# A hybrid decoder layer: its first piece projected by kinds of parts, with keys taken out whole by ScalarE and x in another bank

## Chip, cores and metric

One core of one Trainium2 chip runs the kernel. The metric is the device time of one launch in microseconds: the median of several runs. Profiles are of one execution each, whose time is longer than an unprofiled run's.

## What is computed

One decoder layer over 1024 positions plus 16 meta tokens in front (1040 rows), width 1024, all in float32:

```python
h = concatenate([meta, x])                       # 1040 x 1024
u = rmsnorm(h, g_pre_mix)
q, k, v, xr, yr = split(u @ w_in)                # 512, 128, 128, 512, 512 columns
attn = sliding_window_attention_with_sinks(q, k, v)   # 8 heads, 2 key heads, window 128
hr = rg_lru(causal_depthwise_conv(xr))           # gates, then a scan over time
mix = concatenate([attn, gelu(yr) * hr]) @ w_out
h = h + rmsnorm(mix, g_post_mix)
u = rmsnorm(h, g_pre_ffn)
f = square(relu(u @ w_ff1)) @ w_ff2
out = (h + rmsnorm(f, g_post_ffn))[16:]
```

## The kernel before

**Products in parts.** TensorE multiplies a rounded float32 type. Each operand is therefore kept as two tiles: a high part, which is the value rounded (ScalarE, L95 for weights, L116 for u), and a low part, which is what the rounding left off (VectorE, L98 and L117). A product is three matmuls into the same bank (`mm3`, L123 to L125): high by high, high weight by low u, low weight by high u. The next operation on a bank is its take-out ("sink"): keys, values, queries and x each have one.

**The start.** The rows of h come in as nine tiles: 16 meta rows, then x by 128. `norm_rows` squares a tile on ScalarE with a running sum (L200), GpSimd makes the reciprocal root (L158, L164), VectorE scales the tile (L202). `transposed(b, ...)` turns two such tiles (and meta) into eight blocks of u: TensorE transposes (L242) into a bank of one of the pools pt, o and s in turn, and `split_scaled` writes high and low part (L116, L117). There are four pieces b of 272, 256, 256 and 256 positions. For each piece `project` multiplies with the weights of keys, values, the first query pair and the first x chunk, eight blocks of width times three matmuls each, in a bank of the pool acc:

```python
for b in range(4):
    if b:
        transposed(b, normed(b))
    piece = [ALL[b]]
    project(wk, piece, sink_k)
    project(wv, piece, sink_v)
    project(wq, piece if b else [(16, 256)], sink_q0)
    project(wx, piece, sink_x0)
```

Each pool (acc, s, pt, o) holds two banks. A third use waits until the first is taken out. The keys' take-out (`put_k`, L303 to L305) does, for each of two heads, a copy on ScalarE and a copy and a difference on VectorE; in the first piece it is done once for the 16 meta positions (tile km) and once for the rest.

**After the start.** Attention runs head pair by head pair: scores (reduction on VectorE L467, exponential on ScalarE L82), reciprocals and scalings (L478, L480), transposes of the probabilities (L495) and their high and low parts (L95, L98), products with the values (L506) and their sums (L520, L521). Between them stand "fills": the projections of the other query pairs and of x chunks 1 to 3, which ScalarE copies out by pieces (L339). A chunk's causal convolution is four operations on VectorE (L530, three times L535). Tiles live in slots by tag; the x chunks and their convolutions share the four slots of tag d, so a new chunk's first copy waits for the release of its slot. The gates' weights are loaded into a tile that GpSimd clears first (L604) and four DMAs then fill (L608). Then follow gates, recurrence, output projection and the feed-forward part.

**What sets the order.** The program is written in the order of the source, but the framework's scheduler (`schedule_with_timeline_sim=True`) places the instructions on each engine by priority and its own estimate of times. `behind(name, ins)` adds an order without a semaphore between two instructions of an engine. SP issues the loads in the order that the source has them: meta, two x tiles, gains, weights of keys, values, queries, two x tiles, weights of x, the other x tiles, then small parameters and the next weights.

## Time and profile before

| | |
|---|---|
| median of 3 runs | 974.11 us (974.01 to 975.25) |
| profiled execution | 979.5 us |
| its span, first to last instruction | 977.7 us |
| mean granted TensorE clock | 0.994 |
| TensorE, VectorE, ScalarE, GpSimd busy | 98%, 70%, 51%, 7% of the span |

A row of the timeline is start and duration in us, engine, line, operation, what it writes and reads (buffer numbers left out), its shape and how often it stands there; in brackets the idle time ahead of it and what ended that. PE is TensorE's matmuls, PEld its weight loads, DVE is VectorE, ACT ScalarE, POOL GpSimd, SP the queue that issues most DMAs. Instructions of an engine overlap a little, so the distance of two starts is the price of one in a row, and the duration the time until its result.

### The profile page before, as it was taken

The numbers are of one execution on the slowest core, as the hardware profiler recorded it, in microseconds if no ns is written. First come the engines' busy times: TensorE is split into PE (matmuls) and PEld (weight loads), VectorE is DVE, ScalarE is ACT, GpSimd is POOL, SyncE is SP. The second block draws the span as 40 slices with busy tenths as digits, with TensorE's granted clock in tenths as the row PEclk, the third lists the DMA queues.
The fourth block names the chain that finished last, engine by engine and source line by source line (L and its number), as shares of the span: only waits on it lengthen the run. The fifth ranks groups of instructions, "written<-read, shape, count | busy, mean of one in ns | idle before, by whom it ended". The sixth has DMA issues, their size and how long they took to land.

```text
span 977.7 us, 12515 instructions
## 1 busy us (share of the span) xinstructions
PE 953.8 (98%) x4782; PEld 802.8 (82%) x4782; DVE 680.3 (70%) x1002; ACT 502.4 (51%) x809; POOL 70.4 (7%) x108
## 2 busy tenths in 40 slices
PE   6999999999999999999999999999999999999985
PEld 5999999888878877888888888888888888888874
DVE  6679997765976696675654465476668677779686
ACT  7557673558844664443555565663433444344331
POOL 4100000000011100000000000000111000002012
PEclk9999999999999999999999999999999999999998
DMA  8102101112134457586523364324777766657762
GB/s 275 42 2 65 23 22 44 37 43 73 65 130 155 160 181 236 173 264 191 170 93 103 107 194 129 108 86 129 169 167 182 213 211 200 192 151 197 213 173 86
DMA packets 89371, 133.28 MB, mean 136 GB/s; under 512 B 13752, under 2 KB 52680, under 8 KB 89312
## 3 DMA queue, kind: packets, MB, share of 16 engines
q1 hardware_dynamic: 81488, 112.04, 36.0%
q0 software_dynamic: 6960, 18.35, 8.9%
q10 hardware_dynamic: 864, 2.10, 0.6%
q8 instruction: 37, 0.61, 0.3%
q14 instruction: 22, 0.18, 0.1%
HBM read 113.60 MB, written 18.87 MB: 135 GB/s over the span
## 4 chain that ended last, share of the span: by engine, by line
PE 88%; DVE 5%; DMA 4%; ACT 1%; issue 1%; SPq 0%; POOLq 0%; DVEq 0%; POOL 0%; ACTq 0%
PE ps_acc L124 11%; PE ps_acc L125 11%; PE ps_acc L123 11%; PE ps_s L123 6%; PE ps_s L125 6%; PE ps_s L124 6%; PE ps_pt L123 6%; PE ps_pt L125 6%; PE ps_pt L124 6%; PE ps_o L123 5%; PE ps_o L124 5%; PE ps_o L125 5%; DMA raw<-in_w_ff_dram 3%; PE ps_o L506 2%; PE ps_pt L495 1%; DVE c L650 1%
## 5 line engine op out<-in xcount | busy, mean ns | idle before, releaser
L95 ACT CAST ws<-raw 128x1024 fp32r<-128x1024 f32 (+1 forms) x70 | 71.7, 1024 | 131.2 <-PE ps_o L124 39.8
L98 DVE TENSOR_TENSOR ws<-raw,ws 128x1024 fp32r<-128x1024 f32 (+1 forms) x71 | 84.7, 1194 | 52.7 <-ACT ws L95 52.6
L123 PE MATMUL ps_acc<-a,ws 128*128 128x256 f32 (+2 forms) x272 | 90.5, 333 | 0.6 <-DVE b L305 0.6
L124 PE MATMUL ps_acc<-a,ws 128*128 128x256 f32 (+2 forms) x272 | 89.7, 330 | 0.0
L125 PE MATMUL ps_acc<-a,ws 128*128 128x256 f32 (+2 forms) x272 | 89.4, 329 | 0.0
L95 ACT CAST ws<-e 128x1024 fp32r<-128x1024 f32 x44 | 46.0, 1047 | 61.0 <-PE ps_o L124 28.2
L98 DVE TENSOR_TENSOR b<-b,b 128x1024 fp32r<-128x1024 f32 (+2 forms) x48 | 57.6, 1201 | 25.0 <-PE ps_o L124 17.5
L98 DVE TENSOR_TENSOR ws<-e,ws 128x1024 fp32r<-128x1024 f32 x44 | 53.8, 1223 | 20.3 <-ACT ws L95 20.3
L95 ACT CAST b<-b 128x1024 fp32r<-128x1024 f32 (+2 forms) x48 | 49.4, 1030 | 35.7 <-DVE b L789 33.7
L123 PEld LDWEIGHTS ps_acc<-a,ws 128*128 128x128 f32 x272 | 51.2, 188 | 4.9 <-DVE b L305 0.8
L125 PEld LDWEIGHTS ps_acc<-a,ws 128*128 128x128 f32 x272 | 51.2, 188 | 4.6
L124 PEld LDWEIGHTS ps_acc<-a,ws 128*128 128x128 f32 x272 | 51.2, 188 | 3.9
L123 PE MATMUL ps_acc<-ws,b 128*128 128x512 f32 (+1 forms) x120 | 46.6, 388 | 2.1 <-ACT ws L95 2.1
L124 PE MATMUL ps_acc<-ws,b 128*128 128x512 f32 (+1 forms) x120 | 46.8, 390 | 0.8 <-DVE ws L98 0.8
L125 PE MATMUL ps_acc<-ws,b 128*128 128x512 f32 (+1 forms) x120 | 46.6, 388 | 0.0
L164 POOL TENSOR_TENSOR rs<-ms,half_pow 128x1 f32<-128x1 f32 (+1 forms) x31 | 20.9, 677 | 348.6 <-DVE ms L160 347.2
L123 PE MATMUL ps_pt<-ws,b 128*128 128x512 f32 x112 | 44.1, 394 | 0.0
L124 PE MATMUL ps_pt<-ws,b 128*128 128x512 f32 x112 | 44.1, 394 | 0.0
L125 PE MATMUL ps_pt<-ws,b 128*128 128x512 f32 x112 | 44.0, 393 | 0.0
L123 PE MATMUL ps_s<-ws,b 128*128 128x512 f32 x110 | 43.7, 397 | 0.0
L124 PE MATMUL ps_s<-ws,b 128*128 128x512 f32 x110 | 43.4, 395 | 0.0
L125 PE MATMUL ps_s<-ws,b 128*128 128x512 f32 x110 | 43.3, 393 | 0.0
(375 smaller groups left out, 2676.3 us busy)
## 6 DMA issues: line engine op xcount, KB each, us to landing
raw<-in_w_ff_dram SPq DMA_DIRECT2D x66, 512.0 KB, 3.8
e<-in_w_ff_dram SPq DMA_DIRECT2D x47, 512.0 KB, 3.8
d<-in_w_ff_dram SPq DMA_DIRECT2D x12, 512.0 KB, 4.0
s_dram<-d POOLq DMA_DIRECT2D x12, 512.0 KB, 3.9
raw<-in_w_in_dram SPq DMA_DIRECT2D x9, 512.0 KB, 3.8
raw<-in_w_ff_dram POOLq DMA_DIRECT2D x9, 512.0 KB, 8.0
c<-in_x_dram SPq DMA_DIRECT2D x8, 512.0 KB, 8.6
d<-in_x_dram SPq DMA_DIRECT2D x8, 512.0 KB, 4.5
```

The source lines that it names most:

```text
L95: nc.scalar.copy(hi, src)
L98: low = nc.vector.tensor_tensor(lo, src, f32(hi), op=ALU.subtract).ins
L123: nc.tensor.matmul(dst, lh, rh, start=start, stop=False, skip_group_check=True)
L124: nc.tensor.matmul(dst, lh, rl, start=False, stop=False, skip_group_check=True)
L125: nc.tensor.matmul(dst, ll, rh, start=False, stop=stop, skip_group_check=True)
L164: nc.gpsimd.tensor_tensor(rs[:n], ms[:n], half_pow[:n], op=ALU.pow)
L495: nc.tensor.transpose(pt[:, o : o + P], sn[h][:, 2 * bp + i, s * P : (s + 1) * P], ident,)
L506: nc.tensor.matmul(po[:, oc : oc + n], v, p_[:, pc : pc + n], start=first and k == 0, stop=last and k == 1, skip_group_check=True,)
L650: nc.vector.tensor_tensor_scan(r, av[c], gi, 0.0, op0=ALU.mult, op1=ALU.add)
```

## The change

- The first piece's keys and values are projected by kinds: the keys' eight blocks of high weight by high u, then their eight of high weight by low u, the same two kinds for the values, and only then low weight by high u for both (new function `part`). Queries and x of the first piece follow in the same three kinds, each on its own. The other pieces keep `project`.
- The x projection of the first piece uses a bank of pool s instead of acc. The transposes use the pools as before.
- ScalarE and VectorE each get a fixed order for the first piece (`chained`). ScalarE: high part of the key weights, the eight high parts of u, high part of the value weights, the squares of the next two x tiles, of the query weights; then the keys' take-out, the values', the x weights. VectorE: the eight low parts of u, low parts of key and value weights, the two scalings, low part of the query weights, the keys' take-out, low part of the x weights.
- `put_k` has both ScalarE copies first, then VectorE's four operations; the queries' take-out likewise.
- The tiles khh and kl are made, and kl's halves cleared by GpSimd, ahead of the start's loop.
- The transposes of the later pieces get an order behind the last matmul of an earlier piece through `after`: `done` begins with two empty entries, so piece 1 has none, piece 2 comes behind the first piece's last matmul and piece 3 behind the second's.
- The clearing of the gates' tile comes behind GpSimd's last reciprocal root of the start.

The instructions themselves are the same ones: 4782 matmuls, as many operations on the other engines.

```diff
--- before.py
+++ after.py
@@ -113,16 +113,21 @@
             )
 
     def split_scaled(hi, lo, src, scale):
-        nc.scalar.activation(hi, src, AF.Copy, scale=scale)
-        nc.vector.scalar_tensor_tensor(
+        high = nc.scalar.activation(hi, src, AF.Copy, scale=scale).ins
+        low = nc.vector.scalar_tensor_tensor(
             lo, src, scale, f32(hi), op0=ALU.mult, op1=ALU.subtract
-        )
+        ).ins
+        return high, low
 
     def mm3(dst, lhs, rhs, start, stop):
         (lh, ll), (rh, rl) = lhs, rhs
         nc.tensor.matmul(dst, lh, rh, start=start, stop=False, skip_group_check=True)
         nc.tensor.matmul(dst, lh, rl, start=False, stop=False, skip_group_check=True)
-        nc.tensor.matmul(dst, ll, rh, start=False, stop=stop, skip_group_check=True)
+        last_mm[0] = nc.tensor.matmul(
+            dst, ll, rh, start=False, stop=stop, skip_group_check=True
+        ).ins.name
+
+    last_mm = [None]
 
 
     ident = const.tile([P, P], F32, name="ident")
@@ -161,8 +166,12 @@
                 ms[:n], ssq_parts[0], EPS, ssq_parts[1], op0=ALU.add, op1=ALU.add
             )
         rs = small.tile([P, 1], F32, name="rs", tag="rs")
-        nc.gpsimd.tensor_tensor(rs[:n], ms[:n], half_pow[:n], op=ALU.pow)
+        last_pow[0] = nc.gpsimd.tensor_tensor(
+            rs[:n], ms[:n], half_pow[:n], op=ALU.pow
+        ).ins.name
         return rs[:n]
+
+    last_pow = [None]
 
 
     def load_cols(cols, tag="ws"):
@@ -194,12 +203,18 @@
     u = [pair("a", [P, TT]) for _ in range(KC)]
     RMS_SC = 1.0 / math.sqrt(D)
 
-    def norm_rows(src, n):
+    def norm_rows(src, n, link=False):
         xn = slot("d", [P, D])
         ssq = small.tile([P, 1], F32, name="ssq", tag="ssq")
-        nc.scalar.activation(xn[:n], src, AF.Square, scale=RMS_SC, accum_out=ssq[:n])
+        ins = nc.scalar.activation(
+            xn[:n], src, AF.Square, scale=RMS_SC, accum_out=ssq[:n]
+        ).ins
+        if link:
+            chained(0, ins)
         rs = rstd_of([ssq[:n]], n)
-        nc.vector.tensor_scalar(xn[:n], src, rs, None, op0=ALU.mult)
+        ins = nc.vector.tensor_scalar(xn[:n], src, rs, None, op0=ALU.mult).ins
+        if link:
+            chained(1, ins)
         return xn
 
     def project(w, pieces, sink):
@@ -215,8 +230,26 @@
                 )
             sink(acc[:, :n], t0, n)
 
+
+    def part(acc, w, piece, k, last=2):
+        t0, n = piece
+        for kc in range(KC):
+            last_mm[0] = nc.tensor.matmul(
+                acc[:, :n], w[k // 2][:, kc, :], u[kc][k % 2][:, t0 : t0 + n],
+                start=k == 0 and kc == 0, stop=k == last and kc == KC - 1,
+                skip_group_check=True,
+            ).ins.name
+
     ALL = [(0, 272), (272, 256), (528, 256), (784, 256)]
     REAL2 = [(16, 512), (528, 512)]
+
+
+
+    khh = [slot("b", [P, T], F32R) for _ in range(2)]
+    kl = [slot("b", [P, T], F32R) for _ in range(2)]
+    HALF = (slice(0, HD), slice(HD, P))
+    for h in range(2):
+        nc.gpsimd.memset(f32(kl[h][HALF[1 - h]]), 0.0)
 
     zero = slot("ws", [P, 512])
     nc.vector.memset(zero, 0.0)
@@ -232,22 +265,43 @@
         rows += [(xt[2 * b], P), (xt[2 * b + 1], P)]
         return [(norm_rows(s[:m], m), m) for s, m in rows]
 
-    def transposed(b, xn):
+
+    last = [None, None]
+
+    def chained(e, ins):
+        if last[e] is not None:
+            behind(last[e], ins)
+        last[e] = ins.name
+
+    def high_w(raw, tag="ws"):
+        hi, lo = pair(tag, [P, KC, P])
+        chained(0, nc.scalar.copy(hi, raw).ins)
+        return hi, lo
+
+    def low_w(w, raw):
+        chained(1, nc.vector.tensor_tensor(w[1], raw, f32(w[0]), op=ALU.subtract).ins)
+
+    def transposed(b, xn, after=None):
         t0, n = ALL[b]
         for kc in range(KC):
             flip[0] += 1
             pt = bank(("pt", "o", "s")[flip[0] % 3])
             o = 0
             for s, m in xn:
-                nc.tensor.transpose(
+                ins = nc.tensor.transpose(
                     pt[:, o : o + m], s[:m, kc * P : (kc + 1) * P], ident[:m, :m]
                 )
+                if after:
+                    behind(after, ins.ins)
                 o += m
             uh, ul = u[kc]
-            split_scaled(
+            high = split_scaled(
                 uh[:, t0 : t0 + n], ul[:, t0 : t0 + n], pt[:, :n],
                 g_mix_col[:, kc : kc + 1],
             )
+            if b == 0:
+                chained(0, high[0])
+                chained(1, high[1])
 
     def fetch(cols, tag="raw"):
         raw = slot(tag, [P, KC, P])
@@ -274,11 +328,14 @@
     rx = fetch([(X_COL, P)], "e")
     for i in range(4, 8):
         load_x(i)
-    wk = split_w(rk, "b")
-    wv = split_w(rv, "b")
+    wk = high_w(rk, "b")
     transposed(0, xn)
-    wq = split_w(rq)
-    wx = split_w(rx)
+    low_w(wk, rk)
+    wv = high_w(rv, "b")
+    low_w(wv, rv)
+    xn = [(norm_rows(xt[i], P, True), P) for i in (2, 3)]
+    wq = high_w(rq)
+    low_w(wq, rq)
     nsink = const.tile([P, 8], F32, name="nsink")
     nc.sync.dma_start(nsink, attn_sinks[0].partition_broadcast(P))
     prm_r = slot("d", [8, 512])
@@ -287,38 +344,45 @@
         nc.sync.dma_start(prm_r[4 + i : 5 + i, :], src)
 
 
-
-    khh = [slot("b", [P, T], F32R) for _ in range(2)]
-    kl = [slot("b", [P, T], F32R) for _ in range(2)]
-
     vk = [slot("b", [P, 8, P], F32R) for _ in range(2)]
-    HALF = (slice(0, HD), slice(HD, P))
     vt = slot("c", [P, TT])
-    for h in range(2):
-        nc.gpsimd.memset(f32(kl[h][HALF[1 - h]]), 0.0)
-
-    def put_k(hh, lo, src):
+
+    def put_k(hh, lo, src, link=False):
+        ops = [[], []]
+        for h in range(2):
+            r = HALF[h]
+            ops[0].append(nc.scalar.copy(hh[h][r], src[r]).ins)
         for h in range(2):
             r, o = HALF[h], HALF[1 - h]
-            nc.scalar.copy(hh[h][r], src[r])
-            nc.vector.tensor_copy(hh[h][o], src[r])
-            nc.vector.tensor_tensor(lo[h][r], src[r], f32(hh[h][r]), op=ALU.subtract)
+            ops[1].append(nc.vector.tensor_copy(hh[h][o], src[r]).ins)
+            ops[1].append(
+                nc.vector.tensor_tensor(
+                    lo[h][r], src[r], f32(hh[h][r]), op=ALU.subtract
+                ).ins
+            )
+        if link:
+            for e in range(2):
+                for ins in ops[e]:
+                    chained(e, ins)
 
     def sink_k(acc, t0, n):
         o = 0
         if t0 == 0:
             m = slice(0, NMETA)
             put_k(
-                [km[:, 0, m], km[:, 1, m]], [km[:, 2, m], km[:, 3, m]], acc[:, m]
+                [km[:, 0, m], km[:, 1, m]], [km[:, 2, m], km[:, 3, m]], acc[:, m], True
             )
             o = NMETA
         c = slice(t0 + o - NMETA, t0 - NMETA + n)
         put_k(
-            [khh[0][:, c], khh[1][:, c]], [kl[0][:, c], kl[1][:, c]], acc[:, o:]
+            [khh[0][:, c], khh[1][:, c]], [kl[0][:, c], kl[1][:, c]], acc[:, o:],
+            t0 == 0,
         )
 
     def sink_v(acc, t0, n):
-        nc.scalar.copy(vt[:, t0 : t0 + n], acc)
+        ins = nc.scalar.copy(vt[:, t0 : t0 + n], acc).ins
+        if t0 == 0:
+            chained(0, ins)
 
     def new_q():
 
@@ -327,8 +391,14 @@
         def sink_q(acc, t0, n):
             c = slice(t0 - NMETA, t0 - NMETA + n)
             for h in range(2):
+                r = HALF[h]
+                nc.scalar.activation(q[h][r, c], acc[r], AF.Copy, scale=HD ** -0.5)
+            for h in range(2):
                 r, o = HALF[h], HALF[1 - h]
-                split_scaled(q[h][r, c], q[h][o, c], acc[r], HD ** -0.5)
+                nc.vector.scalar_tensor_tensor(
+                    q[h][o, c], acc[r], HD ** -0.5, f32(q[h][r, c]),
+                    op0=ALU.mult, op1=ALU.subtract,
+                )
 
         return q, sink_q
 
@@ -340,16 +410,39 @@
 
         return xr, sink_x
 
+
+    done = [None, None]
     q0, sink_q0 = new_q()
     xr0, sink_x0 = new_x("c")
     for b in range(4):
         if b:
-            transposed(b, normed(b))
-        piece = [ALL[b]]
-        project(wk, piece, sink_k)
-        project(wv, piece, sink_v)
-        project(wq, piece if b else [(16, 256)], sink_q0)
-        project(wx, piece, sink_x0)
+            transposed(b, xn if b == 1 else normed(b), done[b])
+        piece = ALL[b]
+        if b == 0:
+
+            acc = [bank("acc"), bank("acc")]
+            for a, w in zip(acc, (wk, wv)):
+                part(a, w, piece, 0)
+                part(a, w, piece, 1)
+            for a, w, sink in zip(acc, (wk, wv), (sink_k, sink_v)):
+                part(a, w, piece, 2)
+                sink(a[:, : piece[1]], *piece)
+            wx = high_w(rx)
+            low_w(wx, rx)
+            for w, (t0, n), sink, tag in (
+                (wq, (16, 256), sink_q0, "acc"), (wx, piece, sink_x0, "s")
+            ):
+                acc = bank(tag)
+                for k in range(3):
+                    part(acc, w, (t0, n), k)
+                sink(acc[:, :n], t0, n)
+            done.append(last_mm[0])
+            continue
+        project(wk, [piece], sink_k)
+        project(wv, [piece], sink_v)
+        project(wq, [piece], sink_q0)
+        project(wx, [piece], sink_x0)
+        done.append(last_mm[0])
 
 
     prm = const.tile([P, NLRU, 8], F32, name="prm")
@@ -601,7 +694,7 @@
 
 
     graw = slot("e", [P, 2, NLRU, P])
-    nc.gpsimd.memset(graw, 0.0)
+    behind(last_pow[0], nc.gpsimd.memset(graw, 0.0).ins)
     for i, w in enumerate((w_a, w_x)):
         for s in range(2):
             r = slice(HD * s, HD * s + HD)
```

## The prediction

> **What bounds the kernel now.** I read the busy table first, then TensorE's waits over the whole span, then busy time by stretches, then the timelines of the two places that the change moves. In the waits the columns are the total in us, the number of times and the longest; in the stretches each engine's busy us and instruction count stand in the order PE, PEld, DVE, ACT, POOL, then clock, DMA share and GB/s.
>
> ```profile
> PE 953.8 (98%) x4782; PEld 802.8 (82%) x4782; DVE 680.3 (70%) x1002; ACT 502.4 (51%) x809; POOL 70.4 (7%) x108
> ```
> ```profile
> PE ps_s L242 <- DVE d L202: 5.7, 1, 5.7
> ...
> PE ps_acc L123 <- DVE b L305: 0.6, 1, 0.6
> ```
> ```profile
> 82.00:147.25 65.25, 65.25 (x497) 62.33 (x497) 60.54 (x172) 45.20 (x117) 0.00 (x0) 1.00 0.10 25
> 147.25:156.21 8.96, 8.96 (x79) 8.91 (x78) 8.07 (x9) 2.95 (x8) 0.00 (x0) 1.00 0.21 60
> 156.21:250.00 93.79, 93.79 (x513) 81.92 (x512) 62.07 (x112) 59.13 (x106) 0.00 (x0) 1.00 0.16 46
> ```
>
> TensorE is the bound: 98% busy, and from 82 to 250 us it is never idle, though VectorE is nearly as full between 82 and 156 (60.54 of 65.25 us). So a microsecond of TensorE idle time removed anywhere shortens the span by about as much, and one added lengthens it. What can be gained lies in the start. The change cannot make TensorE's work smaller: the same 4782 matmuls remain.
>
> A second fact decides more than the edits themselves. The kernel's order on each engine is made by a scheduler from priorities. In the changed program TensorE's order differs from the old one up to about matmul 1350 of 4782 (some 200 us) and is the same from there on. So I cost two places: the start, where the edits are, and the rest of those 200 us, where only the order moves.
>
> **The start, part by part.** Rows of the timeline (start, duration, engine, line), the first x rows and key weights, then the second piece:
>
> ```profile
> 7.60 0.75 DVE L202 TENSOR_SCALAR d<-c,rs 128x1024 f32<-128x1024 f32 x1
> 9.06 1.05 ACT L95 CAST b<-raw 128x1024 fp32r<-128x1024 f32 x1 [1.20 <-DMA raw<-in_w_in_dram]
> 9.12 1.52 DVE L202 TENSOR_SCALAR d<-c,rs 128x1024 f32<-128x1024 f32 x1 [0.77 <-POOL rs L164]
> 9.14 2.38 POOL L298 MEMSET b<- 64x1024 f32 x2
> 10.56 2.34 DVE L98 TENSOR_TENSOR b<-raw,b 128x1024 fp32r<-128x1024 f32 x2
> 11.49 0.48 ACT L116 ACTIVATE a<-ps_o,gcol 128x272 fp32r<-128x272 f32 x1
> 11.88 0.48 ACT L116 ACTIVATE a<-ps_s,gcol 128x272 fp32r<-128x272 f32 x1
> 13.24 0.49 DVE L117 SCALAR_TENSOR_TENSOR a<-ps_s,gcol,a 128x272 fp32r<-128x272 f32 x1
> 13.64 0.49 DVE L117 SCALAR_TENSOR_TENSOR a<-ps_pt,gcol,a 128x272 fp32r<-128x272 f32 x1
> 14.53 0.43 PE L123 MATMUL ps_acc<-a,b 128*128 128x272 f32 x1
> 14.75 0.43 PE L124 MATMUL ps_acc<-a,b 128*128 128x272 f32 x1
> 15.88 1.06 ACT L200 ACTIVATE d<-c 128x1024 f32<-128x1024 f32 x1 [0.70 <-PE ps_s L242]
> 18.03 0.75 DVE L202 TENSOR_SCALAR d<-c,rs 128x1024 f32<-128x1024 f32 x1
> 18.37 0.29 PE L124 MATMUL ps_acc<-a,b 128*128 128x272 f32 x1
> 18.49 0.30 PE L125 MATMUL ps_acc<-a,b 128*128 128x272 f32 x1
> ```
> ```profile
> 19.29 1.07 ACT L200 ACTIVATE d<-c 128x1024 f32<-128x1024 f32 x1
> 21.45 0.17 DVE L304 CAST km<-ps_acc 64x16 fp32r<-64x16 f32 x1
> 22.20 0.75 DVE L202 TENSOR_SCALAR d<-c,rs 128x1024 f32<-128x1024 f32 x1 [0.41 <-POOL rs L164]
> 27.23 0.43 DVE L305 TENSOR_TENSOR b<-ps_acc,b 64x256 fp32r<-64x256 f32 x1
> 21.38 0.29 PE L125 MATMUL ps_acc<-a,b 128*128 128x272 f32 x1
> 21.51 0.27 PE L242 MATMUL ps_pt<-ident,d 128*128 128x128 f32 x1
> 21.62 0.27 PE L242 MATMUL ps_o<-ident,d 128*128 128x128 f32 x1
> 22.74 0.36 PE L123 MATMUL ps_acc<-a,ws 128*128 128x256 f32 x1
> 25.53 0.28 PE L125 MATMUL ps_acc<-a,ws 128*128 128x256 f32 x1
> 27.72 0.39 PE L123 MATMUL ps_acc<-a,ws 128*128 128x272 f32 x1 [0.57 <-DVE b L305]
> ```
>
> *Memsets of the key tiles go to the very start of GpSimd's queue.* Today they lie beside the second x row's normalisation, which takes 1.52 us where the first took 0.75. Alone it ends at 9.87 instead of 10.64: 0.77 us earlier. In their new place they stand ahead of the identity and of meta's rstd, which VectorE must have behind it only by 7.60; 2.38 us more on a queue that started at the span's begin leave cover for that, and if it were gone, each microsecond would move the whole start by one. The gates' memset goes behind the eighth rstd; the gate weights' four small DMAs wait for it on SP, and behind them later weight loads. I cost that at nothing: all x rows and the first piece's weights are issued before them, and the attention's projections stand between them and the gates.
>
> *Work by kinds.* ScalarE now does the key weights, then eight high parts of u in a row, and only then the value weights. First high part at about 10.4 instead of 11.49; at a pitch of 0.39 the eight end near 13.6. VectorE does its eight low parts (pitch 0.40) near 10.9 to 14.3 and only then the two weights' low parts (2.34 in all), to 16.6. The value weights' high part is there at 13.6 + 1.05 = 14.6. TensorE takes all 32 products with high weights first (the keys' 16 to about 15.7 at the slow pace of 0.22, 14.53 to 14.75; the values' 16 to about 18.2 while the pace rises to 0.12, 18.37 to 18.49), then the 16 with low weights, 2.0, to 20.2. The old kernel starts its last one at 21.38. Here 1.2 us are won.
>
> *Then it meets a new wait.* The x projection takes its bank from the pool of transposes, and the order that results sends TensorE from eight transposes of the second piece (four banks, near 21.0) straight to one that reuses the first of those banks. That bank is free when VectorE has taken u's low part from it. Ahead of that on VectorE's queue stand: the third and fourth x rows' normalisation, the queries' low weights, four small key copies and the fifth row's normalisation. The third row's square starts at 15.88 in the trace (ScalarE is free from 14.6, but no view shows its data landed sooner), its normalisation 2.15 later (15.88 to 18.03); the fourth's 1.07 behind, 19.1 to 19.9; low weights 1.17, to 21.1; four copies at 0.17, to 21.8; the fifth's normalisation (its square starts at 19.29 and VectorE at 22.20 today; I take 22.0) to 22.7; low part 0.49, to 23.2. TensorE waits some 2 us, then 0.4 more for the next bank, and starts the queries near 23.8, against 22.74 today: +1.1. Both kernels have twelve transposes done there. Behind TensorE's wait stand the queries and all that follows. On ScalarE the fifth square stands ahead of the keys' copies and the second piece's high parts; it lets them go at 20.4, while their transposes are being made.
>
> *The old pause goes.* Today TensorE's last query matmul starts at 25.53 and x starts at 27.72, 2.19 later; 0.12 of that is a matmul and eight transposes at 0.11 (21.51 to 21.62) are work, so 1.19 is idle time, ended by the keys' take-out (L305). With its bank elsewhere x follows at once: -1.2. VectorE's key take-out, four steps of 0.43 to about 26, is then covered by the query and x products (48 at 0.12 = 5.8 us); without this cover it would cost its own 1.7. ScalarE's two copies ahead of VectorE's four change only the order.
>
> Sum of the start: +1.1 - 1.2 = -0.1. Bounds: -1.2 if the new wait is fully absent, +1.3 if the pause is merely moved.
>
> **The rest of the 200 us.** One place shows a price. x chunk 3 is written into the slot that x chunk 2 occupies until its convolution (L530, three times L535) is done. ScalarE's first copy of chunk 3 (L339) waits for that, and TensorE's third piece of chunk 3 waits for the bank that the copy frees:
>
> ```profile
> 140.13 0.48 DVE L467 CUSTOM_DVE_ANT_0 c<-ps_s,mask,nsink 128x256 f32<-128x256 f32 x1
> 140.53 0.48 DVE L467 CUSTOM_DVE_ANT_0 c<-ps_s,mask,nsink 128x256 f32<-128x256 f32 x1
> 141.99 1.15 DVE L480 TENSOR_SCALAR c<-c,rden 128x256 f32<-128x256 f32 x4
> 143.11 0.18 DVE L478 RECIPROCAL rden<-den 128x4 f32<-128x4 f32 x1
> 144.98 0.68 DVE L98 TENSOR_TENSOR c<-ps_pt,c 128x512 fp32r<-128x512 f32 x1
> 153.98 1.29 DVE L535 SCALAR_TENSOR_TENSOR d<-d,prm,d 128x1037 f32<-128x1037 f32 x1
> ```
> ```profile
> 147.25 0.36 ACT L339 COPY d<-ps_acc 128x256 f32<-128x256 f32 x1
> 155.76 0.67 ACT L339 COPY d<-ps_acc 128x272 f32<-128x272 f32 x2
> ```
>
> Today it just fits. From chunk 2's last copy (147.25) VectorE needs 8.0 us to the convolution's end (153.98 + 1.29 = 155.27), then comes the copy, and TensorE starts the piece at 156.21, having been busy with 79 matmuls for all 8.96 us of it. In the new order TensorE has 80 matmuls there, 9.1 us at today's mean; but VectorE has more to do before the convolution's end: four score reductions (pitch 0.40: 1.6), four scalings (1.15), two reciprocals (0.36) and one more low part (0.68), together 3.8. So VectorE needs 8.0 + 3.8 = 11.8, copy and handovers take 0.5 (155.76 to 156.21), and TensorE is let in 12.3 after the last copy: 12.3 - 9.1 = 3.2 us of idle time where there was none. Behind it on TensorE stand the rest of x and the next heads; ScalarE's own queue behind the copy holds only the next copy. VectorE is in order and full there, so the least I allow is 2.0 (a part of the extra work falls into its gaps), the most 3.8 (no slack at all). Elsewhere in these 200 us TensorE has no idle time to give back, so that the reordering is worth 0 there, at most +1 if it makes another wait.
>
> Total: -0.1 + 3.2 + 0 = +3.1 us. The profiled execution took 979.5 (span 977.7 and 1.8 around it), 5.4 over the median; I add the change to each: 982.6 there, 974.1 + 3.1 = **977.2** as the median.
>
> **The rivals.** A difference under 0.2% (1.95 us) is about what a measurement of this kernel can't tell from none.
>
> *The convolution is covered after all* and the start is a wash: 974.1. For it: today's slack is only just used up, and 3.8 us of small steps could shift in time. Against: these steps stand ahead of the convolution's end on an in-order queue. 0.11.
>
> *The start gains and nothing is lost later* (ends on the other side): the second piece's wait is not there, 974.1 - 1.2 = 972.9. It turns on whether the fifth row's normalisation is over on VectorE before about 21. Against: its square does not start before 19.29. 0.06. The same gain with the later loss, 974.1 - 1.2 + 3.2 = 976.1, is at the edge of no change: 0.06.
>
> *The array's fast pace comes later.* Matmuls of 272 columns follow at 0.22 us near 14.5 and at 0.12 near 18.4. In the new order TensorE is fed at ScalarE's pitch of 0.39 until 13.6 and so is less dense. If the slow pace lasts until 20, some 30 products of 0.10 more each cost 3.0, of which the 2 us wait hides two thirds: +1.0, hence 978.2. 0.12. The Trainium skill (TensorE: Matmul & The Clock Gate, "What's actually happening") says that the array starts at half clock and is released after a window of about 3.4 us of sustained work, whose phase is free. The trace agrees with a release near 16.5, and cannot show the phase of another run.
>
> *Another wait arises in the reordered stretch*, of about 2 us: 979.2. VectorE's 60.54 of 65.25 us speaks for it; nothing names a place. 0.05.
>
> **How the numbers follow.** Forecast 0.60, at 977.2. Slower: 0.60 + 0.12 + 0.05 = 0.77; same 0.11 + 0.06 = 0.17; faster 0.06. Range: low 974.1 + 2.5 - 1.2 = 975.4 (the start gains, the convolution costs 2.5, midway to its least), high 974.1 + 3.8 + 1.2 = 979.1 (both near their worst). Below it lie the first two rivals, 0.17; above it the last.
>
> **What would show it.** Right: the second x row's normalisation takes 0.75; TensorE's first wait in the second piece is at a transpose (L291 of the changed kernel) for VectorE's low part near 21 to 23 us; no wait at x's first product; a wait of 2 to 3.5 us near 155 us at a matmul for ScalarE's copy of x. Wrong: TensorE without idle time from 82 to 250 us, as before; or queries starting before 22.7.

## The result, and the profile after

The changed kernel takes 982.47 us (median of 7 executions, 981.8 to 987.2) where the kernel before, run beside it, takes 975.65, 6.8 us less. A second series gave 986.45 (6 executions) against 977.75, 8.7 us. The ratios on record, which are not simply those of two medians, are 1.0063 (95% interval 1.0035 to 1.0090) and 1.0089 (1.0063 to 1.0114). The change makes the kernel slower, as forecast, and by about twice the 3.1 us that were forecast, or more.

TensorE's waits over the whole span of the changed kernel (total, times, longest), the two of the prediction:

```profile
PE ps_pt L291 <- DVE a L117: 2.5, 1, 2.5
PE ps_acc L124 <- ACT d L409: 2.0, 1, 2.0
```

Both are there. What the prediction did not have is in the next view: busy time by stretches, cut at the moments at which the granted clock changes (busy us and count for PE, PEld, DVE, ACT, POOL, then clock, DMA share, GB/s). First the changed kernel:

```profile
10.25:13.66 3.41, 3.41 (x16) 2.86 (x15) 2.95 (x7) 2.84 (x8) 0.00 (x0) 1.00 1.06 339
13.66:16.74 3.08, 3.08 (x25) 2.89 (x25) 2.63 (x3) 3.08 (x5) 0.60 (x1) 1.00 1.06 368
...
20.49:23.90 3.41, 0.87 (x7) 0.55 (x6) 3.27 (x10) 3.37 (x9) 0.98 (x1) 1.00 0.67 158
23.90:27.32 3.42, 3.42 (x18) 3.42 (x18) 3.33 (x7) 0.78 (x3) 0.00 (x0) 0.50 0.62 174
150.20:153.61 3.41, 3.37 (x30) 3.13 (x29) 3.35 (x10) 1.65 (x5) 0.00 (x0) 1.00 0.00 0
153.61:157.02 3.41, 1.39 (x12) 1.25 (x11) 3.41 (x8) 1.60 (x4) 0.00 (x0) 1.00 0.02 5
157.02:160.44 3.42, 3.42 (x18) 3.42 (x17) 1.38 (x5) 0.00 (x0) 0.00 (x0) 0.50 0.00 0
```

Behind each wait stands one stretch of 3.41 us at a clock of 0.50: 18 matmuls lie in it where 30 lie in the full stretch at 150.20. Half of 3.41 is 1.7 us of TensorE's work. The kernel before has no such stretch in these places; it has one of its own near the end, which the prediction passed over (of its mean clock of 0.994 this stretch is the smaller part: from 969.06 on, with the matmuls done, the clock is at 0.50 as well). Its stretches there, its waits from 900 to 960, and the cast that ends the first:

```profile
928.10:931.51 3.41, 0.87 (x5) 0.34 (x3) 0.95 (x1) 1.99 (x2) 0.00 (x0) 1.00 0.05 10
931.51:934.92 3.41, 3.08 (x7) 2.48 (x8) 3.41 (x6) 1.21 (x2) 0.00 (x0) 0.50 0.52 164
```
```profile
PE ps_acc L123 <- ACT ws L95: 2.1, 1, 2.1
PE ps_acc L124 <- DVE ws L98: 0.8, 1, 0.8
```
```profile
921.03 1.18 POOL L1050 DMA_DIRECT2D raw<-in_w_ff_dram  x1 [12.73 <-DVE ws L98]
...
929.48 1.04 ACT L95 CAST ws<-raw 128x1024 fp32r<-128x1024 f32 x1 [6.57 <-DMA raw<-in_w_ff_dram]
```

A weight of the last product is loaded in two parts, the second by an accumulating load on GpSimd's queue. Issued at 921.03 it landed 8.4 us later; TensorE waits 2.9 us and then works at half clock, 4.8 us in all, by what this trace loses between matmuls 4600 and 4650 to the changed kernel's first trace, which does not have this wait. There the load is issued 2.9 us earlier against matmul 4600 and lands in 5.5. The changed kernel's second trace has the wait. That is why the two profiled spans, 977.7 and 979.9, differ by only 2.2.

To see where the time goes, each trace's n-th matmul is set against the n-th of the kernel before's first trace (all have 4782). The order is the same from matmul 1434 on, in x3b and "both" from 1502 on; up to there a row compares equal counts of matmuls, not the same products. Positive is later, in us; "x3b", "banks" and "both" are the repairs below:

| matmul, its time before | changed | changed, again | x3b | banks | both |
|---|---|---|---|---|---|
| 74, first keys and values done, 21.6 | -2.17 | -2.86 | -2.46 | -2.76 | -2.65 |
| 84, queries begin, 22.7 | +1.01 | +0.55 | +0.85 | -2.70 | -2.59 |
| 110, queries done, 25.8 | +2.56 | +1.52 | +2.10 | -1.70 | -1.69 |
| 172, second piece, 34.4 | +1.26 | +0.25 | +0.81 | -2.98 | -2.97 |
| 1000, 142 | +1.40 | +0.36 | +0.93 | -2.92 | -2.92 |
| 1085, 152 | +3.86 | +2.82 | +1.03 | -0.47 | -2.82 |
| 1360, 198 | +5.07 | +4.06 | +0.42 | +0.64 | -3.42 |
| 4600, 928 | +6.99 | +5.59 | +1.25 | +3.13 | -2.63 |
| 4781, 967 | +2.20 | +7.44 | -0.14 | +0.50 | -2.05 |

Most of the loss is made in two places, at 21 to 27 us and at 142 to 198; another 1.9 and 1.5 us come between 198 and 928. The last row mixes in the wait near 930, which the reference trace has and the first trace of the changed kernel has not.

### The profile page after: what moved, and what is told of

It is laid out like the page before. It is cut to its first block, busy times and chain, and to the rows that moved or that the text cites. A ratio compares the mean times of both kernels' runs of the same rounds, so it can differ in the third digit from the quotient of the medians.

```text
span 979.9 us, 12533 instructions
## 1 busy us (share of the span) xinstructions
PE 955.7 (98%) x4782; PEld 803.9 (82%) x4782; DVE 680.5 (69%) x1002; ACT 502.2 (51%) x809; POOL 71.6 (7%) x108
## 4 chain that ended last, share of the span: by engine, by line
PE 91%; DVE 5%; ACT 2%; issue 1%; POOL 1%; POOLq 0%; DVEq 0%
PE ps_acc L124 11%; PE ps_acc L125 11%; PE ps_acc L126 11%; PE ps_s L126 6%; PE ps_s L124 6%; PE ps_s L125 6%; PE ps_pt L124 6%; PE ps_pt L125 6%; PE ps_pt L126 6%; PE ps_o L125 5%; PE ps_o L124 5%; PE ps_o L126 5%; PE ps_o L599 2%; PE ps_pt L588 1%; PE ps_acc L237 1%; DVE c L743 1%
## 5 line engine op out<-in xcount | busy, mean ns | idle before, releaser
L124 PE MATMUL ps_acc<-a,ws 128*128 128x256 f32 (+2 forms) x256 | 86.4, 337 | 2.0 <-ACT d L409 2.0
L125 PE MATMUL ps_acc<-a,ws 128*128 128x256 f32 (+2 forms) x256 | 85.9, 336 | 0.0
L126 PE MATMUL ps_acc<-a,ws 128*128 128x256 f32 (+2 forms) x256 | 85.8, 335 | 0.0
L95 ACT CAST ws<-e 128x1024 fp32r<-128x1024 f32 x42 | 43.9, 1044 | 58.6 <-PE ps_o L125 32.7
L98 DVE TENSOR_TENSOR ws<-e,ws 128x1024 fp32r<-128x1024 f32 x42 | 51.3, 1222 | 19.9 <-ACT ws L95 19.9
L124 PEld LDWEIGHTS ps_acc<-a,ws 128*128 128x128 f32 x256 | 49.0, 192 | 6.1 <-ACT d L409 2.2
L126 PEld LDWEIGHTS ps_acc<-a,ws 128*128 128x128 f32 x256 | 48.9, 191 | 4.4
L125 PEld LDWEIGHTS ps_acc<-a,ws 128*128 128x128 f32 x256 | 49.0, 191 | 3.9
```

What stands on the lines that cost most here:

```text
L95: nc.scalar.copy(hi, src)
L98: low = nc.vector.tensor_tensor(lo, src, f32(hi), op=ALU.subtract).ins
L124: nc.tensor.matmul(dst, lh, rh, start=start, stop=False, skip_group_check=True)
L125: nc.tensor.matmul(dst, lh, rl, start=False, stop=False, skip_group_check=True)
L126: last_mm[0] = nc.tensor.matmul(dst, ll, rh, start=False, stop=stop, skip_group_check=True).ins.name
```

## The experiments

**Pauses alone.** A kernel that holds nothing but dense blocks of matmuls with pauses between them; its output is not the layer's.

```python
for m in range(10):                       # six times over
    for i in range(n):                    # 96 to 110 matmuls of 256 columns
        nc.tensor.matmul(acc[:, 0:256], w, s, start=i == 0, stop=i == n - 1, ...)
    nc.vector.tensor_scalar(t[:, 0:256], acc[:, 0:256], ...)
    ...                                   # m more steps on VectorE, then s, the next operand
```

> Not the layer: TensorE alone runs 60 dense blocks of 96 to 110 matmuls of 256 columns; between two blocks VectorE takes the result out and back through 2 to 11 small steps, so TensorE is idle for about 0.9 to 3.5 us (ten lengths, six times each). The output is not the layer's. Theory A (a half-clock window follows an idle time of about 2 us): pauses under about 1.5 us leave the granted clock at 1.0, pauses of about 2 to 3.5 us are each or mostly followed by one stretch of 3.41 us at 0.5. Rival B (only idle time that fills a whole window of 3.41 us lowers the clock): none of these pauses, or the longest alone, shows a 0.5. Rival C (the 0.5 stretches of the layer have nothing to do with the pauses): 0.5 stretches fall without regard to the length of the pause.

Stretches of it, cut on the grid on which its clock changes:

```profile
73.76:77.18 3.42, 1.26 (x11) 1.06 (x10) 1.89 (x6) 0.00 (x0) 0.00 (x0) 1.00 0.00 0
77.18:80.59 3.41, 3.41 (x18) 3.41 (x17) 0.00 (x0) 0.00 (x0) 0.00 (x0) 0.50 0.00 0
391.20:394.62 3.42, 1.75 (x15) 1.54 (x13) 1.50 (x5) 0.00 (x0) 0.00 (x0) 1.00 0.00 0
394.62:398.03 3.41, 2.92 (x24) 2.93 (x25) 0.40 (x2) 0.00 (x0) 0.00 (x0) 1.00 0.00 0
398.03:401.44 3.41, 3.41 (x31) 3.41 (x30) 0.00 (x0) 0.00 (x0) 0.00 (x0) 1.00 0.00 0
299.04:302.46 3.42, 1.56 (x14) 1.36 (x12) 1.65 (x6) 0.00 (x0) 0.00 (x0) 1.00 0.00 0
302.46:305.87 3.41, 1.80 (x15) 1.80 (x16) 1.42 (x5) 0.00 (x0) 0.00 (x0) 1.00 0.00 0
305.87:309.29 3.42, 3.42 (x31) 3.42 (x30) 0.00 (x0) 0.00 (x0) 0.00 (x0) 1.00 0.00 0
```

The same pause of 2.16 us lies wholly in one stretch at 74 us, which leaves it 1.26 busy, and the next runs at 0.50. At 393 it is cut by the grid, 1.67 and 0.49, and the clock stays. Even 3.47 us at 300, cut 1.86 and 1.61, does nothing. The 59 pauses go by one rule: behind a stretch of 3.41 us at full clock of which over 0.55 was idle the next is at half clock each time, behind one with up to 0.533 never; of four in between, three at 0.536 are followed by it and one at 0.543 is not. Where a half-clock stretch itself holds some of the pause, a second can follow. By length: none of 18 pauses up to 1.58 us; 3 of 6 at 1.83, 2 of 6 at 2.16, 3 of 6 at 2.48, 5 of 6 at 2.81, 6 of 6 at 3.14, 5 of 6 at 3.47, all 5 at 3.80. Theory A stands, sharpened: not the length counts, but the share of one stretch. B and C fall.

The Trainium skill (TensorE: Matmul & The Clock Gate, "What's actually happening") gives a free-running window of 3413 ns and puts the fall to half rate "after ≥1 idle window (~3.4µs)". The window is what the traces show, on a grid that lies differently in each run. The idle window is not: 1.83 us of idle time did it.

**Each wait taken away, and both.** x chunk 3 in a slot that no convolution holds ("x3b"), the banks of the first piece's queries and x swapped ("banks"), and both:

```diff
-            xr, sink = new_x()
+            xr, sink = new_x("b" if c == 3 else "d")
```
```diff
-                (wq, (16, 256), sink_q0, "acc"), (wx, piece, sink_x0, "s")
+                (wq, (16, 256), sink_q0, "s"), (wx, piece, sink_x0, "acc")
```

> The changed kernel with x chunk 3 written into a slot that no convolution holds. Theory A (each wait costs its idle time and a window of 3.41 us at half clock behind it, worth 1.7): the wait of 2.0 us near 155 and the 0.5 stretch from 157.0 go, 3.7 us off the changed kernel's 982.5: 978.8. Rival B (the wait alone counts): 2.0 off, 980.5. Rival C (the slot is not what TensorE waits for): a wait for ScalarE's copy remains near 155, 982.5. The wait of 2.5 us at the second piece's transpose and its 0.5 stretch stay in all three.

> The changed kernel with the two banks of the first piece swapped: its queries go into a bank of the pool s, its x projection into a bank of acc. Theory A: the wait of 2.5 us at the second piece's transpose and the 0.5 stretch from 23.9 go, 4.2 us off 982.5: 978.3. Rival B (idle time alone): 2.5 off, 980.0. Rival C (the bank only moves the wait to another instruction, since VectorE's queue is what is late): the idle time and the time stay, 982.5. The wait of 2.0 us near 155 stays in all three.

> The changed kernel with both edits: banks of the first piece swapped, and x chunk 3 in the other slot. Theory A (both waits and both half-clock stretches go): 4.5 us of idle time and 3.4 of half clock off 982.5, 974.6, about 1 under the 975.7 of the kernel before. Rival B (idle time alone): 978.0, slower than the kernel before. Rival C (what makes the changed kernel slow is the order, not the two waits): it stays over 980.

| kernel | median us | ratio to before, beside it | interval |
|---|---|---|---|
| changed | 982.47; 986.45 | 1.0063; 1.0089 | 1.0035 to 1.0090; 1.0063 to 1.0114 |
| x3b | 980.73 | 1.0029 | 1.0005 to 1.0053 |
| banks | 980.62 | 1.0032 | 1.0011 to 1.0054 |
| both | 976.09 | 0.9993 | 0.9973 to 1.0014 |

Each repair removes its wait and its half-clock stretch from the trace and leaves the other; with both, no wait over 0.8 us is left between 10 and 900 us. By the ratios (times 977.5, the median of the kernel before in this series), the changed kernel's two series lie on average 7.4 over the kernel before, x3b 2.8, banks 3.1, both -0.7. So the repairs are worth 4.6, 4.3 and 8.1, where A had 3.7, 4.2 and 7.9, and B 2.0, 2.5 and 4.5. Each interval is some 2 to 2.6 us to either side, so it is the pair together that speaks against B. About 1 us of what x3b and "both" gain is neither the wait nor its clock: from 198 to 928 us they lose 0.8, the changed kernel 1.9 and 1.5, "banks" 2.5. The table of matmuls agrees: x3b goes from +0.93 to +0.42 between matmuls 1000 and 1360 where the changed kernel goes from +1.40 to +5.07, a difference of 4.2, of which 2.4 come up to matmul 1085, with the wait, and 1.8 behind it. This place decides between A and B, since it holds one wait and what follows it.

"Both" was forecast below the kernel before and came out the same: 2.6 us ahead at 928, it has waits for the weight near 930 too, with a half-clock stretch from 930.05:

```profile
PE ps_acc L124 <- ACT ws L95: 2.5, 1, 2.5
...
PE ps_acc L125 <- DVE ws L98: 0.8, 1, 0.8
```

The trace that it is set against has this wait as well, so "both" still ends 2.05 ahead of it; the medians are over executions with and without the wait. x3b has almost the same wait there (1.9 and 0.8), cut by the grid:

```profile
927.39:930.81 3.42, 2.31 (x16) 1.94 (x14) 0.00 (x0) 0.33 (x1) 0.00 (x0) 1.00 0.72 131
930.81:934.22 3.41, 1.89 (x7) 1.36 (x8) 2.67 (x3) 1.66 (x2) 0.00 (x0) 1.00 0.11 14
934.22:937.63 3.41, 3.41 (x20) 2.86 (x19) 3.41 (x5) 1.77 (x3) 0.70 (x1) 1.00 0.81 285
```

Idle shares of 0.32 and 0.45, no half clock, and from matmul 4600 to 4650 it gains 1.56 on the kernel before, whose wait is 0.2 longer: some 1.4 is what that one's half-clock stretch cost.

**The changed kernel once more**, for a second trace.

> The changed kernel as it is, a second trace. Theory A (a half-clock stretch follows only where more than about 0.54 of a window of 3.41 us is idle, and the windows lie by chance): the waits of 2.5 us near 23 and 2.0 us near 155 are there again, within 0.3; the 0.5 stretches behind them come each in somewhat over half of the executions, so each may be there or not; a wait for weights near 930 may appear, as in the traces of the kernel before and of the repaired kernels. Time 980 to 985. Rival D (the waits themselves vary from run to run): the two waits differ by over 0.5.

The waits are 2.5 and 2.0 again: D falls. Both half-clock stretches are there as well, at 21.92 and 155.04, and near 930 a wait of 2.9 and 0.5 followed by two of them. At the start the half-clock stretch began while TensorE still waited, so less work fell into it: from matmul 84 to 110 it loses 0.97 where the first trace lost 1.55.

**x back in a bank of acc**, the rest of the change kept.

```diff
-                (wq, (16, 256), sink_q0, "acc"), (wx, piece, sink_x0, "s")
+                (wq, (16, 256), sink_q0, "acc"), (wx, piece, sink_x0, "acc")
```

> The changed kernel with its x projection of the first piece back in a bank of acc; everything else of the change stays. TensorE's wait for VectorE in the second piece should shrink to about 1.6, under the shortest pause (1.83) behind which a half-clock stretch was seen, and the one near 155 should go or split into pieces under 0.9. Theory A (idle time and half-clock stretches): 1.7 us less idle time and 1.7 to 3.4 less from the clock: 979.1 to 977.4 against the changed kernel's 982.5. Rival B (idle time alone): 980.8. Rival C (the bank of x has no part in it): 982.5.

979.78, ratio 1.0025 (1.0005 to 1.0046). The wait at the transpose was sized wrongly: it is still 2.3, with a half-clock stretch from 24.0. The one near 155 is gone but for two of 0.4 at most, as expected, and with it its stretch: at matmul 1360 it is 1.96 late against 5.07 and 4.06. So C falls: the bank of the first piece's x reorders what comes 130 us later, and here the wait for chunk 3 goes with it. The bank alone does not decide this: in the kernel before the same bank brings no such wait (below), and "banks" keeps the wait though its x is in acc and its queries are in s. It isn't what makes the wait at the start.

**An attempt to cut the pause at the start in two.**

```diff
-        return [(norm_rows(s[:m], m), m) for s, m in rows]
+        return [(norm_rows(s[:m], m, after=lows[3] if b else None), m) for s, m in rows]
```

This is the main line of it: `after` puts a row's normalisation on VectorE behind the fourth low part of the piece before.

> The changed kernel in which the normalisation of a later piece's rows stands on VectorE behind four low parts of the piece before. The idle time at the start stays about the same, 1.8 us, but in two pieces of 1.2 and 0.7 with matmuls between, neither long enough for a half-clock stretch by itself. Theory A: the 0.5 stretch near 24 is gone although the idle time is not, and TensorE is 0.7 to 2.4 us earlier than the changed kernel at the first piece's end (x done); time about 980.8. Rival B (idle time alone): 0 to 0.7 us earlier there, 982. The wait near 155 stays in both.

It did not cut the pause, so it tells nothing of A against B: one wait of 1.8 remained, the stretch from 19.38 to 22.79 was 1.62 busy, and the half clock followed. 985.24, ratio 1.0074 (1.0045 to 1.0102), the changed kernel's own.

**x's bank alone, in the kernel before.**

```diff
-        project(wx, piece, sink_x0)
+        project(wx, piece, sink_x0, "acc" if b else "s")
```

> The kernel before with one part of the change alone: x's first piece in a bank of pool s. Theory A: TensorE's pause of 0.6 to 1.2 us at x's first product (L123, for L305) goes, no wait for VectorE in the second piece takes its place, and up to 155 us TensorE is some 0.6 to 1.2 us ahead of the kernel before; small waits of 0.4 to 0.7 near 154, below any that lowered the clock, take this back. Rival C (x in this bank is what brings the wait at the second piece's transpose): a wait of about 2 us there.

There is one execution, 980.45 us, so its trace alone counts. The pause at x's first product is gone and no wait of 2 us at a transpose takes its place, so C falls; from matmul 110 to 143 it gains 1.35, is 0.49 ahead at matmul 172 and 0.82 behind at 1360. By itself this part brings nothing that lasts.

**The wait near 930.** Its weight loaded by SP into a tile of its own and added by VectorE, in the kernel before and in "both"; then the same for all three accumulating loads of the last product; and the kernel before once more.

```diff
-                q % 3 < 2 if i < 6 else q in (0, 2, 4)
+                q % 3 < 2 if i < 6 else q in (0, 4)
```
```diff
-                q % 3 < 2 if i < 6 else q in (0, 2, 4)
+                i < 6 and q % 3 < 2
```

> The kernel before as it is, a second trace. Theory A: the clock is released behind the first window of 3.41 us in which TensorE was idle for less than about a tenth, near 13 to 18 us; no 0.5 stretch before 900 us; the wait for weights near 930 (2.1 and 0.8 us in the first trace) is there or not, and if over half of one window is idle there a 0.5 stretch follows. Rival D (the 0.5 stretches are thrown at random): some fall between 30 and 900.

> The kernel before, and in its last product's third step the second weight is loaded by SP into a tile of its own and added by VectorE, where GpSimd's accumulating load added it behind the first. Nothing of the first 900 us changes. Theory A (the wait near 930 is this accumulating load, which landed 8.4 us after its issue where there was a wait and 5.5 where there was none): the wait of 2.1 + 0.8 us and its 0.5 stretch go, and the executions that lay at 977 to 982 come to 974 to 976: median 975. Rival E (the wait is for the queue of loads as a whole): it stays or moves to the next step, median 977 to 978.

> The changed kernel with both its waits removed (first piece's banks swapped, x chunk 3 in the other slot) and the same edit of the last product's third step. Without it, this kernel was 2.6 us ahead of the kernel before at 928 us and lost 3.3 us of idle time and 1.7 of clock behind. Theory A: about 972 to 974, the median 3 to 5 under the kernel before. Rival E: 976, as without the edit.

> As the run before, with all three accumulating loads of the last product replaced by pairs of SP's loads. Theory A: as that one, 972 to 974, if loads by SP are nowhere later than GpSimd's. Rival E: SP's queue, which also carries the output's stores, becomes what is late: a wait at another step of the last product and 976 to 979.

The second trace of the kernel before waits 2.2 and 0.8 there and has a half-clock stretch from 931.7, and none before 900: D falls. With the edit this wait is in no trace, and no other takes its place: E falls. The kernel before then takes 975.2 to 978.0, median 976.52, where beside it the unedited one takes 973.8 to 983.2, median 978.43: the long executions are gone, the shortest became 1.4 longer, and the ratio, 0.9987 (0.9966 to 1.0007), is not told apart from 1. A's 975 was too good by what the edit costs at the very end: it also puts VectorE's last operations in another order, and from the last matmul's start to the end of the span it takes 12.6 us instead of 11.2 (13.7 with all three loads replaced). "Both" with the edit takes 973.89 (973.2 to 975.6), ratio **0.9957** (0.9940 to 0.9974): 4.2 us faster than the kernel before by this ratio, and the fastest kernel here. With the same edit in both, the repaired change is worth 2.6 us (976.52 to 973.89, 12 executions each in one series), as much as it is ahead at 928 without it. With all three loads replaced it is 975.21, 0.9970 (0.9953 to 0.9988). In "both" with the one edit, the three places lie like this:

```profile
20.49:23.90 3.41, 2.73 (x23) 2.53 (x22) 3.21 (x10) 2.59 (x6) 0.64 (x2) 1.00 0.53 125
153.61:157.02 3.41, 3.41 (x24) 3.07 (x23) 1.54 (x3) 1.32 (x2) 0.00 (x0) 1.00 0.00 0
928.10:931.51 3.41, 3.41 (x21) 2.93 (x20) 3.41 (x5) 1.13 (x2) 3.00 (x2) 1.00 0.58 158
```

## Why the prediction was wrong

**The step that failed** is the price of a wait. The prediction holds that "a microsecond of TensorE idle time removed anywhere shortens the span by about as much, and one added lengthens it", and so its sum charged both new waits with their idle time alone. Behind each stands a half-clock stretch, a term that the sum put at nothing: it cost 1.55 and 0.97 us at the start and 1.21 and 1.24 behind the wait for x chunk 3, in the two traces of the changed kernel. Up to 928 us those traces are 7.0 and 5.6 later where +3.1 was forecast:

| part | forecast | first trace | second trace |
|---|---|---|---|
| start, to matmul 172 | -0.1 | +1.26 | +0.25 |
| x chunk 3, matmuls 1000 to 1360 | +3.2 | +3.67 | +3.70 |
| elsewhere, to matmul 4600 | 0 | +2.06 | +1.64 |

Of the 5.3 us between 977.2 and 982.47, 3.7 are the change and 1.5 the base, 974.11 where 975.65 was measured beside it.

**The wait at the start was right, step by step.** VectorE's and then TensorE's timeline of the changed kernel:

```profile
8.82 0.75 DVE L215 TENSOR_SCALAR d<-c,rs 128x1024 f32<-128x1024 f32 x1 [0.77 <-POOL rs L169]
...
19.16 0.75 DVE L215 TENSOR_SCALAR d<-c,rs 128x1024 f32<-128x1024 f32 x1 [0.76 <-POOL rs L169]
19.83 1.22 DVE L282 TENSOR_TENSOR ws<-e,ws 128x1024 fp32r<-128x1024 f32 x1
21.07 0.17 DVE L357 CAST km<-ps_acc 64x16 fp32r<-64x16 f32 x1
...
21.84 0.75 DVE L215 TENSOR_SCALAR d<-c,rs 128x1024 f32<-128x1024 f32 x1
22.62 0.48 DVE L117 SCALAR_TENSOR_TENSOR a<-ps_pt,gcol,a 128x256 fp32r<-128x256 f32 x1
```
```profile
20.35 0.27 PE L291 MATMUL ps_o<-ident,d 128*128 128x128 f32 x1
23.16 0.44 PE L291 MATMUL ps_pt<-ident,d 128*128 128x128 f32 x2 [2.54 <-DVE a L117]
23.55 0.44 PE L291 MATMUL ps_o<-ident,d 128*128 128x128 f32 x2
23.75 4.62 PE L237 MATMUL ps_acc<-a,ws 128*128 128x256 f32 x24
28.20 2.15 PE L237 MATMUL ps_s<-a,ws 128*128 128x272 f32 x16
```

The second x row's normalisation takes 0.75. The fourth row's came at 19.16 (forecast 19.1), the low part that lets TensorE go ended at 23.10 (23.2), the queries begin at 23.75 (23.8), and x follows them without a wait. The old pause gave back 1.24 and 1.22 (1.2 forecast), from matmul 110 to 143. What fails is the sum of -0.1: the 24 query matmuls take 4.5 us, from 23.75 to 28.20, because nearly all of them run at half clock. That term, +1.55 and +0.97 in the two traces (matmuls 84 to 110), was not in the sum.

**The wait for x chunk 3 was right in kind and 1.2 too long.** The last copy of chunk 2, the convolution's end, chunk 3's first copies and TensorE's piece:

```profile
144.13 0.37 ACT L409 COPY d<-ps_acc 128x256 f32<-128x256 f32 x1
...
154.12 1.29 DVE L628 SCALAR_TENSOR_TENSOR d<-d,prm,d 128x1037 f32<-128x1037 f32 x1
...
155.45 0.66 ACT L409 COPY d<-ps_acc 128x272 f32<-128x272 f32 x2 [0.87 <-DVE d L628]
155.89 0.39 PE L124 MATMUL ps_acc<-a,ws 128*128 128x256 f32 x1 [2.02 <-ACT d L409]
```

TensorE is let in 11.8 us after the last copy (forecast 12.3) and needs 9.7 of them for its own work (9.1), so 2.0 is left (3.2). VectorE's part was sized 0.5 too long: the convolution ends 11.3 after that copy, not 11.8. In place, from matmul 1000 to 1085, the delay is 2.46 in both traces. Then the half clock is added; to matmul 1360 the place costs 3.67 and 3.70. The two errors, the wait too long and the half clock left out, nearly cancel, so it is luck that 3.2 comes near the total here.

**"Elsewhere 0" did not hold.** From 198 to 928 us, in an unchanged order, the changed kernel loses 1.9 and 1.5 more. One piece of it is single, 0.5 near 747 in the first trace, with a wait of 0.2 for a weight's low part; the rest comes in many small steps. They go with the program and not with the execution: from matmul 2300 to 2900 the two traces lose 0.80 and 0.81, "banks" 0.94, x3b and "both" 0.13 each. What makes them was not tried and stays open.

**The base was misread.** The prediction took the 5.4 us between the profiled execution and the median of three as going with the profile. 4.8 of it is the wait near 930 with its half-clock stretch. All three traces with the kernel before's loads and its order there (two of itself, one with x's bank alone) have it, and by the times many executions do: in a series of 29 the kernel before ran from 974.0 to 982.0 around a median of 977.54, the ten executions with a mean clock of 0.995 or less from 977.5 to 982.0, the nineteen with more from 974.0 to 979.6. Nor is a profiled execution longer as such: those of x3b and "banks", 979.48 and 980.15, lie under their medians. Three executions of 974.0 to 975.3, by their times without that wait, were a poor base, and 974.1 + 3.1 a poor sum even where 3.1 held.

**The rivals.** "The array's fast pace comes later" had the sign wrong: the first stretch without idle time at the start, or next to none, ends at 13.66 and 11.68 in the changed kernel's traces (see 10.25:13.66 above) and at 16.74 in the kernel before. There the first clock record stands, so the 1.00 that the view prints for stretches ahead of it is no reading:

```profile
9.91:13.33 3.42, 2.19 (x9) 1.64 (x8) 3.42 (x5) 2.98 (x7) 1.56 (x2) 1.00 1.03 283
13.33:16.74 3.41, 3.37 (x15) 3.05 (x16) 3.41 (x7) 2.71 (x5) 0.96 (x1) 1.00 1.01 357
16.74:20.15 3.41, 3.41 (x29) 3.41 (x29) 2.02 (x4) 3.41 (x7) 1.68 (x4) 1.00 1.03 416
```

The count of matmuls nearly doubles behind it in both (x16 to x25 within 3.08 us in the one, x15 to x29 in the other). Work by kinds does feed TensorE more densely, and keys and values are done 2.2 to 2.9 us earlier instead of 1.2; the wait for VectorE then eats it, since the queries' start is set by VectorE. Where the banks are swapped, this gain stays: -2.97 at matmul 172. "The convolution is covered", "the start gains" and "another wait" did not come.

## What to carry to other kernels

A wait of a tensor engine that is otherwise always busy is to be priced with what its clock does behind it: look for stretches at half clock in the profile of before, and add half a window where more than about half of one window is idle; two short waits apart can cost less than one long one. A profiled execution that lies several us over the median is to be read for a wait that only some executions have before its span is used as a base. A tile's bank or slot should be chosen by whose queue lets it go: the swap of two banks and one slot turned this change from 7 us slower to no slower than before, and to 2.6 us faster where the wait near 930 is gone from both kernels.

## What was not expected of the hardware

The granted clock falls for idle times well under a window: some 0.54 of 3.41 us, or 1.83 us, is enough if they lie in one window, and 3.47 us can be harmless if they are cut. In the layer the bound is nearly the same: the full-clock windows followed by half clock were idle for 0.52 or more, those idle for 0.50 or less were not followed by it (the ends of matmuls are modelled, so the second figure is rough).

A load that adds to a tile on GpSimd's queue took between 5.5 and 8.4 us to land in the same place of the program. Nine of the ten traces with this load wait there, for 1.6 to 3.4 us; in the one that does not, it landed soonest and was also issued earliest against the matmuls around it.
